# Cross-entropy backward: from two DMA queues and whole rows to one queue and sets of every fourth partition

## The chip, the cores and the metric

The kernel runs on one core of a Trainium2 chip. The metric is device time in microseconds. Before the change it is 1248.48, the median of three runs from 1247.92 to 1248.65. A profile of one further execution, with its trace, belongs to it.

## The reference

The gradient of a cross-entropy loss with respect to the logits: a softmax over the vocabulary, less one at the label.

```python
# logits: (8, 1024, 8192) float32, labels: (8, 1024) int32
logits_max = np.max(logits, axis=-1, keepdims=True)
exp_logits = np.exp(logits - logits_max)
softmax = exp_logits / np.sum(exp_logits, axis=-1, keepdims=True)
one_hot[batch_idx, seq_idx, labels] = 1.0
return (softmax - one_hot).astype(np.float32)
```

The logits are 268 MB, and as much is written.

## The kernel before

The 8192 rows are cut into `B` = 32 blocks of 256 rows. A block lies on 128 partitions with `G` = 2 rows each: partition p holds rows 2p and 2p + 1 of the block, which are neighbours in memory, 32 KB each. The text calls the 128 first rows "row t0" and the 128 second ones "row t1" (64 such row steps, t = 0 to 63). The buffer `X` has `SLOTS` = 3 slots of one block; block b uses slot b % 3, and the result overwrites the logits in place. So block b + 3 can be loaded only where block b has been stored.

A row step has four parts.

- `row_max(t)`: VectorE (DVE) takes the negated maximum of 8192 elements, after the load has landed.
- `exponentials(t)`: ScalarE (ACT) replaces the row by its exponentials and sums them.
- `mark(t)`: ACT prepares the one-hot of the label in PSUM (`hot`), in two instructions: the distance of each position from the label's word, and from this a word with one byte set. There are two buffers, one per parity of t, so `mark(t + 2)` waits for `finish(t)`.
- `finish(t)`: DVE takes the reciprocal of the sum, then multiplies the row by it and subtracts the one-hot. The last two rows are finished in two halves each.

Each block's order is written out by hand. The string `ORDER` is "r" throughout: maximum of t1, finish of t0, exponentials of t1, store of t0, mark, then already the next block's first maximum, finish of t1, the next block's exponentials, store of t1, mark, and last the load of block b + 3.

Transfers go on two queues. Loads are issued by SyncE (SP), the stores by ACT. The string `LOADS` tells how a block is loaded: "s" (blocks 0 to 2) row by row in two sets of every second partition, one on SP and one on ACT; "r" row by row over all partitions; "w" the whole block in one transfer of 8 MB, where a partition's two rows are one stretch of 64 KB. `STORES` is "r" throughout. A load waits for the stores of the block three earlier that touch the same partitions and rows (`meets`). The last two rows are stored in two halves, on SP and on ACT. Every engine works in its order, so an instruction that waits holds up all behind it on the same engine.

All operations are recorded by the helper `run`, so the profile shows nearly everything at its line, L76 (L75 for a wait that stands alone).

Of the kernel before, what the change touches and what calls it, by code (L numbers as in the profile page):

```python
# [7 lines left out]
P = 128  # L8
G = 2
SLOTS = 3  # L10

LOADS = "sssrrwwwwwwwwwwwwwwwwwwwwwwwwrrr"
STORES = "rrrrrrrrrrrrrrrrrrrrrrrrrrrrrrrr"
ORDER = "rrrrrrrrrrrrrrrrrrrrrrrrrrrrrrrr"


@with_exitstack
def kernel(
# [6 lines left out]
    nc = tc.nc  # L25
# [11 lines left out]
    T = N // P  # L37
    B = T // G
# [3 lines left out]
    o_b = o_nv.rearrange("(b p j) v -> b p j v", p=P, j=G)  # L42
# [4 lines left out]
    X = const.tile([P, SLOTS, G, V], fp32)  # L47
# [11 lines left out]
    m, s, r = (const.tile([P, T], fp32, name=n) for n in ("m", "s", "r"))  # L59
# [4 lines left out]
    with tc.tile_critical():  # L64
        sem = tc.alloc_semaphore
        got = [[sem(f"got{i}{q}") for q in range(4)] for i in range(SLOTS)]
        put = [[sem(f"put{i}{q}") for q in range(4)] for i in range(SLOTS)]
# [3 lines left out]
        def run(engine, waits, counter, method, **operands):  # L71

            waits = list(dict.fromkeys(waits))
            for w in waits[:-1]:
                engine.wait_ge(*w)  # L75
            instruction = getattr(engine, method)(**operands)  # L76
            for w in waits[-1:]:
                instruction._wait_ge(*w)
            step = 16 if method == "dma_start" else 1
            instruction.then_inc(counter, step)  # L80
            count[counter.name] = count.get(counter.name, 0) + step
            return counter, count[counter.name]

        every, rows = slice(0, P), slice(0, G)
        one = [slice(j, j + 1) for j in range(G)]
        halves = [slice(i, P, 2) for i in range(2)]
        sides = [slice(i * V // 2, (i + 1) * V // 2) for i in range(2)]
        PIECES = {
            "r": [(every, js) for js in one],
            "s": [(ps, js) for js in one for ps in halves],  # L90
            "w": [(every, rows)],
        }

        def meets(a, b):
# [3 lines left out]
        loaded, stored, sides_done = {}, {}, {}  # L98
        maxed, summed, marked, finished, freed = {}, {}, {}, {}, {}

        def load(b):
            loaded[b] = []
            before = stored.get(b - SLOTS, [])
            for q, piece in enumerate(PIECES[LOADS[b]]):
                ps, js = piece
                free = [w for other, w in before if meets(piece, other)]
                queue = nc.scalar if LOADS[b] == "s" and ps == halves[1] else nc.sync
                w = run(
                    queue, free, got[b % SLOTS][q], "dma_start",
                    out=X[ps, b % SLOTS, js, :], in_=x_b[b, ps, js, :],  # L110
                )
                loaded[b].append((piece, w))

        def store(t):
            b, j = divmod(t, G)
            stored.setdefault(b, [])
            if t >= T - G:
                for i, cs in enumerate(sides):
                    w = run(
                        nc.sync if t == T - G else nc.scalar, [sides_done[t][i]], put[b % SLOTS][G * j + i],  # L120
                        "dma_start", out=o_b[b, every, one[j], cs], in_=X[every, b % SLOTS, one[j], cs],
                    )
                    stored[b].append(((every, one[j]), w))
                return
            for q, piece in enumerate(PIECES[STORES[b]]):
                ps, js = piece
                if js.stop != j + 1:
                    continue
                w = run(
                    nc.scalar, [finished[t]], put[b % SLOTS][q], "dma_start",  # L130
                    out=o_b[b, ps, js, :], in_=X[ps, b % SLOTS, js, :],
                )
                stored[b].append((piece, w))

        def row(t):
            return X[:, t // G % SLOTS, t % G, :]
# [4 lines left out]
        def row_max(t):  # L141
            b, j = divmod(t, G)
            arrived = {w[0].name: w for piece, w in loaded[b] if meets(piece, (every, one[j]))}
            maxed[t] = run(
                nc.vector, arrived.values(), dve, "tensor_reduce",
                out=m[:, t : t + 1], in_=row(t), axis=mybir.AxisListType.X, op=Alu.max, negate=True,
            )

        def exponentials(t):
            w = run(  # L150
                nc.scalar, [maxed[t]], act, "activation",
                out=row(t), in_=row(t), func=Act.Exp, bias=m[:, t : t + 1], scale=1.0,
                accum_out=s[:, t : t + 1],
            )
            summed[t] = w

        def mark(t):
            if t >= T:
                return
            w = run(  # L160
                nc.scalar, ([made] if t < G else [freed[t - G]]) + ([marked[t - 1]] if t else []), act, "activation",
                out=away[:], in_=count16[:], func=Act.Abs, bias=at(word, t), scale=1.0,
            )
            marked[t] = run(
                nc.scalar, [w], act, "activation",
                out=hot[:, t % G, :], in_=away[:], func=Act.Relu, bias=at(unit, t), scale=at(minus, t),
            )

        def finish(t):
            w = run(nc.vector, [summed[t]], dve, "reciprocal", out=r[:, t : t + 1], in_=s[:, t : t + 1])  # L170
            bytes_ = hot[:, t % G, :].bitcast(u8)
            sides_done[t] = []
            for i, c in enumerate(sides if t >= T - G else [slice(0, V)]):
                last = run(
                    nc.vector, [marked[t], w] if i == 0 else [], dve, "scalar_tensor_tensor",
                    out=row(t)[:, c], in0=row(t)[:, c], scalar=r[:, t : t + 1], in1=bytes_[:, c],
                    op0=Alu.mult, op1=Alu.subtract,
                )
                sides_done[t].append(last)
            finished[t] = freed[t] = last  # L180

        w_raw = run(nc.scalar, [], lab_got, "dma_start", out=lab_raw[:], in_=lab_bp)
        for b in range(SLOTS):
            load(b)
        w = run(nc.gpsimd, [], pool, "memset", ap=ident[:], constant=0.0)
        w_ident = run(
            nc.gpsimd, [w], pool, "affine_select",
            out=ident[:], in_=ident[:], compare_op=Alu.not_equal, fill=1.0,
# [8 lines left out]
        for j in range(G):  # L197
            w = run(
                nc.tensor, [w_ident, w_lab], pe, "transpose",
                out=lab_ps[:, j, :], in_=lab_f[:, j, :], identity=ident[:],  # L200
            )
        w = run(nc.vector, [w], dve, "tensor_copy", out=lab[:], in_=lab_ps)
        w = run(
            nc.vector, [w], dve, "tensor_scalar",
            out=part[:], in0=lab[:], scalar1=2, scalar2=None, op0=Alu.arith_shift_right,
        )
        w_word = run(
            nc.vector, [w], dve, "tensor_scalar",
            out=word[:], in0=part[:], scalar1=-1.0, scalar2=None, op0=Alu.mult,
        )  # L210
        w = run(
            nc.vector, [w_word], dve, "tensor_scalar",
            out=lab[:], in0=lab[:], scalar1=3, scalar2=None, op0=Alu.bitwise_and,
        )
        w = run(
            nc.vector, [w], dve, "tensor_copy", out=minus[:], in_=lab[:]
        )
# [3 lines left out]
            out=unit[:], in0=minus[:], scalar1=0.0, scalar2=powers[0], op0=Alu.is_equal, op1=Alu.mult,  # L221
# [21 lines left out]
        mark(1)  # L243
        for b in range(B):
            t0, t1 = b * G, b * G + 1
            nxt = t1 + 1
            if ORDER[b] == "b":
                if t0 not in maxed:
                    row_max(t0)
                    exponentials(t0)  # L250
                row_max(t1)
                exponentials(t1)
                finish(t0)
                store(t0)
                mark(t0 + G)
                finish(t1)
                store(t1)
                mark(t1 + G)
                if b + SLOTS < B:
                    load(b + SLOTS)  # L260
                continue
            if t0 not in maxed:
                row_max(t0)
                exponentials(t0)
            row_max(t1)
            finish(t0)
            exponentials(t1)
            store(t0)
            mark(t0 + G)
            ahead = nxt < T and ORDER[b + 1] == "r"  # L270
            if ahead:
                row_max(nxt)
            finish(t1)
            if ahead:
                exponentials(nxt)
            store(t1)
            mark(t1 + G)
            if b + SLOTS < B:
                load(b + SLOTS)
        for b in range(B - SLOTS, B):  # L280
            for _, w in stored[b]:
                nc.scalar.wait_ge(*w)
# [30 lines left out]
```

## Time and profile before

| | |
|---|---|
| timed runs, median of 3 | 1248.48 us (1247.92 to 1248.65) |
| profiled execution, first to last instruction (span) | 1246.6 us |
| DVE busy | 1120.2 us, 90% |
| ACT busy | 722.7 us, 58% |
| moved by DMA | 536.98 MB in 15413 packets, mean 431 GB/s |
| DMA issues | 113: loads 46, stores 66, labels 1 |

The page gives no time for the profiled execution but its span; the timed runs lie about 1.9 us above it. In the page, q1 is the queue on which SP issues and q10 the one on which ACT issues; both feed the same sixteen DMA engines. "Share of 16 engines" is the time that a queue's packets took, over sixteen times the span or the stretch asked for. A packet is counted in the stretch in which it starts, so in a short stretch the shares can add up to more or less than 100%. The chain lists the work that ended last, followed back from the end.

### The profile page before, as it was taken

What the parts mean: (1) busy time and instruction counts of PE and PEld (TensorE: products, weight loads), DVE (VectorE), ACT (ScalarE), POOL (GpSimd) and SP (SyncE); (2) the same over time, 40 slices, a digit from 0 to 9 for tenths busy, and PEclk for the clock granted to TensorE, in tenths of its full rate; (3) what the DMA queues carried; (4) which work ended last, traced back from release to release, by engine and by line L of the source; (5) the groups of instructions that cost most, each with busy time, mean ns of one, the idle gap of its engine ahead of it and who ended that gap; (6) DMA issues with size and microseconds to landing.
All of it is one profiled execution on the core that took longest, in us unless ns stands there. A gap on an engine that the chain in (4) does not pass through costs nothing.

```text
span 1246.6 us, 809 instructions
## 1 busy us (share of the span) xinstructions
PE 0.4 (0%) x2; PEld 0.3 (0%) x2; DVE 1120.2 (90%) x208; ACT 722.7 (58%) x257; POOL 2.3 (0%) x7
## 2 busy tenths in 40 slices
PE   0000000000000000000000000000000000000000
PEld 0000000000000000000000000000000000000000
DVE  5999998889988889888898888998889988899995
ACT  2866664556555565465655655556556555566662
POOL 0000000000000000000000000000000000000000
DMA  9999999999999999999999999999999999999998
GB/s 406 413 431 434 437 432 444 435 437 421 433 429 437 443 423 433 434 431 435 430 441 435 422 435 435 434 440 426 432 434 431 433 446 434 422 430 435 429 434 383
DMA packets 15413, 536.98 MB, mean 431 GB/s; under 512 B 1808, under 2 KB 1808, under 8 KB 1840
## 3 DMA queue, kind: packets, MB, share of 16 engines
q10 hardware_dynamic: 9744, 276.89, 51.5%
q1 hardware_dynamic: 5664, 260.05, 48.3%
q14 instruction: 5, 0.04, 0.0%
HBM read 268.50 MB, written 268.44 MB: 431 GB/s over the span
## 4 chain that ended last, share of the span: by engine, by line
DMA 59%; DVE 26%; issue 11%; ACT 3%; DVEq 0%; ACTq 0%; SPq 0%
DMA X<-in_logits_dram 33%; DMA out_dram<-X 26%; DVE X L76 15%; DVE m L76 10%; ACT X L76 2%; DVEq L64 0%; DVE r L76 0%; ACT hot L76 0%; ACT away L76 0%; ACTq L76 0%; DVEq L75 0%; ACTq L308 0%; SPq L64 0%
## 5 line engine op out<-in xcount | busy, mean ns | idle before, releaser
L76 ACT ACTIVATE X<-X,m 128x8192 f32<-128x8192 f32 x64 | 455.8, 7122 | 365.2 <-DVE m L76 365.2
L76 DVE TENSOR_REDUCE m<-X 128x1 f32<-128x8192 f32 x64 | 555.6, 8682 | 105.4 <-DMA X<-in_logits_dram 105.4
L76 DVE SCALAR_TENSOR_TENSOR X<-X,r,hot 128x8192 f32<-128x8192 f32 (+1 forms) x66 | 560.1, 8489 | 3.8 <-ACT hot L76 1.6
L76 ACT ACTIVATE away<-count,word 128x2048 bf16<-128x2048 int16 x64 | 128.1, 2001 | 127.0 <-DVE X L76 127.0
L76 ACT ACTIVATE hot<-away,unit,minus 128x2048 int32<-128x2048 bf16 x64 | 131.9, 2061 | 2.1
L76 ACT ACTIVATION_READ_ACCUMULATOR X<-X,m 128x1 f32 x64 | 11.9, 186 | 0.0
L76 DVE RECIPROCAL r<-s 128x1 f32<-128x1 f32 x64 | 9.8, 153 | 0.0
L76 ACT ACT_TABLE_LOAD x1 | 1.3, 1283 | 5.3 <-issue 5.3
L76 DVE CAST lab_f<-lab_raw 32x256 f32<-32x256 int32 x1 | 0.5, 536 | 2.7 <-DMA lab_raw<-in_labels_dram 2.7
L76 POOL IOTA count<- 128x2048 int16 x1 | 1.8, 1823 | 0.0
L76 DVE TENSOR_TENSOR unit<-unit,part 128x64 f32<-128x64 f32 x3 | 0.7, 225 | 0.1
L76 DVE CAST lab<-hot 128x64 int32<-128x64 f32 x1 | 0.2, 224 | 0.5 <-PE hot L76 0.5
L76 DVE TENSOR_SCALAR part<-minus 128x64 f32<-128x64 f32 x3 | 0.6, 194 | 0.1
L76 PE MATMUL hot<-ident,lab_f 32*128 32x32 f32 x2 | 0.4, 298 | 3.3 <-DVE lab_f L76 3.3
L76 PEld LDWEIGHTS hot<-ident,lab_f 32*128 32x128 f32 x2 | 0.3, 192 | 3.3 <-DVE lab_f L76 3.3
L76 DVE CAST minus<-lab 128x64 f32<-128x64 int32 x1 | 0.2, 195 | 0.0
L76 DVE TENSOR_SCALAR word<-part 128x64 f32<-128x64 int32 x1 | 0.2, 195 | 0.0
L76 DVE TENSOR_SCALAR lab<-lab 128x64 int32<-128x64 int32 x1 | 0.2, 195 | 0.0
L76 DVE TENSOR_SCALAR unit<-minus 128x64 f32<-128x64 f32 x1 | 0.2, 195 | 0.0
L76 DVE TENSOR_SCALAR part<-lab 128x64 int32<-128x64 int32 x1 | 0.2, 194 | 0.0
L76 DVE TENSOR_SCALAR minus<-unit 128x64 f32<-128x64 f32 x1 | 0.2, 194 | 0.0
L76 POOL TENSOR_SCALAR_AFFINE_SELECT ident<-ident 32x32 f32<-32x32 f32 x1 | 0.2, 203 | 0.1
(5 smaller groups left out, 0.5 us busy)
## 6 DMA issues: line engine op xcount, KB each, us to landing
out_dram<-X ACTq DMA_DIRECT2D x62, 4096.0 KB, 30.4
X<-in_logits_dram SPq DMA_DIRECT2D x10, 4096.0 KB, 28.1
X<-in_logits_dram SPq DMA_DIRECT2D x6, 2048.0 KB, 32.6
X<-in_logits_dram ACTq DMA_DIRECT2D x6, 2048.0 KB, 37.1
out_dram<-X SPq DMA_DIRECT2D x2, 2048.0 KB, 12.7
out_dram<-X ACTq DMA_DIRECT2D x2, 2048.0 KB, 11.9
X<-in_logits_dram SPq DMA_DIRECT2D x24, 33.4
lab_raw<-in_labels_dram ACTq DMA_DIRECT2D x1, 64.0 KB, 1.8
```

The costliest lines, as they stand in the source:

```text
L76: instruction = getattr(engine, method)(**operands)
```

## The change

- All loads of logits and all stores are issued by SP. ACT issues only the load of the labels.
- Blocks 0 to 2 are loaded row by row over all partitions ("r"). All later blocks are loaded, and blocks 0 to 28 are stored, in four sets ("q"): set q holds the partitions q, q + 4, q + 8 and so on, 32 of them, with both rows, 2 MB. The last three blocks are stored by rows, and the very last one in halves of rows.
- `move(b)` runs once per block, after both rows are finished. It issues the stores of block b and the loads of block b + 3 in the order of `TURN`. The load of set q waits for the store of set q alone.
- The computation goes by block: both maxima and exponentials, then both finishes and marks. The next block's first maximum no longer comes ahead of the second finish.

```diff
-LOADS = "sssrrwwwwwwwwwwwwwwwwwwwwwwwwrrr"
-STORES = "rrrrrrrrrrrrrrrrrrrrrrrrrrrrrrrr"
-ORDER = "rrrrrrrrrrrrrrrrrrrrrrrrrrrrrrrr"
+SETS = 4
+TURN = [('S', 0), ('S', 1), ('L', 0), ('S', 2), ('L', 1), ('S', 3), ('L', 2), ('L', 3)]
+LOADS = "rrrqqqqqqqqqqqqqqqqqqqqqqqqqqqqq"
+STORES = "qqqqqqqqqqqqqqqqqqqqqqqqqqqqqrrr"
...
-        halves = [slice(i, P, 2) for i in range(2)]
+        sets = [slice(i, P, SETS) for i in range(SETS)]
...
-            "s": [(ps, js) for js in one for ps in halves],
-            "w": [(every, rows)],
+            "q": [(ps, rows) for ps in sets],
...
-        def load(b):
+        def load(b, only=None):
...
             for q, piece in enumerate(PIECES[LOADS[b]]):
+                if only is not None and q != only:
+                    continue
                 ps, js = piece
                 free = [w for other, w in before if meets(piece, other)]
-                queue = nc.scalar if LOADS[b] == "s" and ps == halves[1] else nc.sync
                 w = run(
-                    queue, free, got[b % SLOTS][q], "dma_start",
+                    nc.sync, free, got[b % SLOTS][q], "dma_start",
...
-        def store(t):
+        def store(b, only=None):
...
                 w = run(
-                    nc.scalar, [finished[t]], put[b % SLOTS][q], "dma_start",
+                    nc.sync, [finished[b * G + js.stop - 1]], put[b % SLOTS][q], "dma_start",
                     out=o_b[b, ps, js, :], in_=X[ps, b % SLOTS, js, :],
                 )
...
+        def move(b):
+            if b + SLOTS >= B:
+                store(b)
+                return
+            for what, q in TURN:
+                if what == "S":
+                    store(b, q)
+                else:
+                    load(b + SLOTS, q)
...
             row_max(t1)
+            exponentials(t1)
             finish(t0)
-            exponentials(t1)
-            store(t0)
             mark(t0 + G)
-            ahead = nxt < T and ORDER[b + 1] == "r"
-            if ahead:
-                row_max(nxt)
             finish(t1)
-            if ahead:
-                exponentials(nxt)
-            store(t1)
             mark(t1 + G)
-            if b + SLOTS < B:
-                load(b + SLOTS)
+            move(b)
```

More of the change, by code (lines that the diff above doesn't have):

```diff
@@ L99 @@
         maxed, summed, marked, finished, freed = {}, {}, {}, {}, {}
-        def load(b):
-            loaded[b] = []
+        def load(b, only=None):
+            loaded.setdefault(b, [])
             before = stored.get(b - SLOTS, [])
             for q, piece in enumerate(PIECES[LOADS[b]]):
+                if only is not None and q != only:
+                    continue
                 ps, js = piece
                 free = [w for other, w in before if meets(piece, other)]
-                queue = nc.scalar if LOADS[b] == "s" and ps == halves[1] else nc.sync
                 w = run(
-                    queue, free, got[b % SLOTS][q], "dma_start",
+                    nc.sync, free, got[b % SLOTS][q], "dma_start",
                     out=X[ps, b % SLOTS, js, :], in_=x_b[b, ps, js, :],
@@ L112, in load @@
                 loaded[b].append((piece, w))
-        def store(t):
-            b, j = divmod(t, G)
+        def store(b, only=None):
             stored.setdefault(b, [])
[L117 to L123, printed above, removed]
+            if b == B - 1:
+                for t in (T - G, T - 1):
+                    j = t % G
+                    for i, cs in enumerate(sides):
+                        w = run(
+                            nc.sync, [sides_done[t][i]], put[b % SLOTS][G * j + i],
+                            "dma_start", out=o_b[b, every, one[j], cs], in_=X[every, b % SLOTS, one[j], cs],
+                        )
+                        stored[b].append(((every, one[j]), w))
                 return
             for q, piece in enumerate(PIECES[STORES[b]]):
+                if only is not None and q != only:
+                    continue
                 ps, js = piece
-                if js.stop != j + 1:
-                    continue
                 w = run(
-                    nc.scalar, [finished[t]], put[b % SLOTS][q], "dma_start",
+                    nc.sync, [finished[b * G + js.stop - 1]], put[b % SLOTS][q], "dma_start",
                     out=o_b[b, ps, js, :], in_=X[ps, b % SLOTS, js, :],
@@ L245 @@
             t0, t1 = b * G, b * G + 1
[L246 to L251, printed above, removed]
-                exponentials(t1)
-                finish(t0)
-                store(t0)
-                mark(t0 + G)
-                finish(t1)
-                store(t1)
-                mark(t1 + G)
-                if b + SLOTS < B:
-                    load(b + SLOTS)
-                continue
             if t0 not in maxed:
@@ L265 @@
             row_max(t1)
+            exponentials(t1)
             finish(t0)
-            exponentials(t1)
-            store(t0)
             mark(t0 + G)
-            ahead = nxt < T and ORDER[b + 1] == "r"
-            if ahead:
-                row_max(nxt)
             finish(t1)
-            if ahead:
-                exponentials(nxt)
-            store(t1)
             mark(t1 + G)
-            if b + SLOTS < B:
-                load(b + SLOTS)
+            move(b)
         for b in range(B - SLOTS, B):
```

## The prediction

> **What bounds the kernel now.** The page first: its head, engine shares, DMA slices, queues and chain.
>
> ```profile
> span 1246.6 us, 809 instructions
> PE 0.4 (0%) x2; PEld 0.3 (0%) x2; DVE 1120.2 (90%) x208; ACT 722.7 (58%) x257; POOL 2.3 (0%) x7
> DMA  9999999999999999999999999999999999999998
> DMA packets 15413, 536.98 MB, mean 431 GB/s; under 512 B 1808, under 2 KB 1808, under 8 KB 1840
> q10 hardware_dynamic: 9744, 276.89, 51.5%
> q1 hardware_dynamic: 5664, 260.05, 48.3%
> DMA 59%; DVE 26%; issue 11%; ACT 3%; DVEq 0%; ACTq 0%; SPq 0%
> ```
>
> DVE looks busiest among the engines at 90%, but the two DMA queues together held all sixteen DMA engines for 51.5 + 48.3 = 99.8% of the span. Queue q1 is SP's and q10 is ACT's. So the bytes set the time, not a chain of waits. The chain that ended last (the fence's last line, 59% DMA and 26% DVE) only tells whom each block waited for.
>
> How long is a packet? The DMA view, cut to two stretches. From 276.0 to 279.6 only stores were moving, from 279.4 to 281.0 the first packets of the next load began:
>
> ```profile
> q10 hardware_dynamic: 48, 1.57, 101.1%
> ...
> q1 hardware_dynamic: 16, 1.05, 151.2%
> ```
>
> A store packet has 1.57 MB / 48 = 32 KB and took 1.011 x 3.6 x 16 / 48 = 1.213 us; a load packet has 64 KB and took 1.512 x 1.6 x 16 / 16 = 2.419 us. (A packet is counted where it starts, so a share can pass 100%.) Direction doesn't matter, only bytes, and a large packet saves next to nothing: 2 x 1.213 - 2.419 = 0.007 us.
>
> Now the work of one DMA engine, counted from the code, each of the sixteen taking 8 of a row's 128 packets. Loads: eight blocks in 32 KB packets, 128 of them, and 24 blocks in 64 KB packets, 192. Stores: 62 rows, 496 of 32 KB, and two rows in 16 KB packets, worth 32 x 0.61. That is 624 x 1.213 + 192 x 2.419 + 19.5 = 1240.9 us. Beside these stand 1808 packets under 512 B, 16 for each of 113 transfers. A stretch from 58.69 to 61.9, used again below, prices them:
>
> ```profile
> q10 hardware_dynamic: 32, 1.05, 104.9%
> q1 hardware_dynamic: 16, 0.00, 0.3%
> ```
>
> 16 of them took 0.003 x 3.21 x 16 / 16, about 0.01 us each. With 113 x 0.008 (the 0.3% is rounded) the sum is 1241.8 us. The other 4.8 us of the span are its two ends, in the windows:
>
> ```profile
> 0.00:2.00 2.00, 0.00 (x0) 0.00 (x0) 0.00 (x0) 0.00 (x0) 1.18 (x7) 1.00 0.02 7
> ...
> 1240.00:1245.00 5.00, 0.00 (x0) 0.00 (x0) 0.00 (x0) 0.00 (x0) 0.00 (x0) 1.00 0.68 292
> 1245.00:1247.00 2.00, 0.00 (x0) 0.00 (x0) 0.00 (x0) 0.00 (x0) 0.00 (x0) 1.00 0.00 0
> ```
>
> 2 us before the first data, 1.6 us after 1245, and (1 - 0.68) x 5 = 1.6 us while some DMA engines had finished and others not. 1241.8 + 5.2 is 0.4 over the span; the account closes. The timed runs' median, 1248.48, is 1.9 above this span; I take that offset as kept.
>
> **The change part by part.** *Packets.* All stores of 29 blocks and all loads of 29 blocks become 64 KB packets: 464 x 2.419 = 1122.4. Left in 32 KB packets are three blocks of loads and two of stores, 80 x 1.213 = 97.0, and the last block's 19.5. Sum 1238.9, a gain of 2.0 us. Transfers grow from 113 to 6 + 232 + 4 + 4 + 1 = 247, so the small packets cost 247 x 0.008 = 2.0, 1.1 more. Net: **-0.9 us**; if a small packet is 0.01, -0.6.
>
> *Sets of every fourth partition.* 32 partitions are two packets per engine if all sixteen share them equally. No row shows such a set. The nearest are the first loads of before, in sets of every second partition, from 20 to 44 us:
>
> ```profile
> DMA packets 396, 10.42 MB, mean 434 GB/s; under 512 B 78, under 2 KB 78, under 8 KB 78
> ```
>
> 434 GB/s, against 431 for the whole: stride 2 costs nothing, and I take nothing for stride 4.
>
> *Order by block.* The groups give DVE's and ACT's instructions:
>
> ```profile
> L76 ACT ACTIVATE X<-X,m 128x8192 f32<-128x8192 f32 x64 | 455.8, 7122 | 365.2 <-DVE m L76 365.2
> L76 DVE TENSOR_REDUCE m<-X 128x1 f32<-128x8192 f32 x64 | 555.6, 8682 | 105.4 <-DMA X<-in_logits_dram 105.4
> L76 DVE SCALAR_TENSOR_TENSOR X<-X,r,hot 128x8192 f32<-128x8192 f32 (+1 forms) x66 | 560.1, 8489 | 3.8 <-ACT hot L76 1.6
> L76 ACT ACTIVATE away<-count,word 128x2048 bf16<-128x2048 int16 x64 | 128.1, 2001 | 127.0 <-DVE X L76 127.0
> L76 ACT ACTIVATE hot<-away,unit,minus 128x2048 int32<-128x2048 bf16 x64 | 131.9, 2061 | 2.1
> L76 DVE RECIPROCAL r<-s 128x1 f32<-128x1 f32 x64 | 9.8, 153 | 0.0
> ```
>
> A block on DVE: two maxima, then two finishes, 2 x 8.68 + 2 x 8.75 + 2 x 0.15 = 35.2 us (8.75 is 560.1 / 64). The exponentials (7.1 plus 0.2 each) lie under the second maximum and the first finish; ACT's marks, 2 x 4.1, lie under the second finish and the next maximum. DVE has no gap of its own. DMA needs 16 packets x 2.419 = 38.7 us per block, so DVE has 3.5 to spare. The start: six row loads fill SP's queue from 2 us to 60.2 (48 x 1.213). Row 1 is there at 21.4, its maximum ends at 30.1; ACT does the first two marks before the second exponential, 27.7 to 35.9, so that one ends at 43.2, and the second finish at 52.1. The first store is therefore issued 8 us before the queue runs dry. Block 1 is done at 87.3 and needed at 98.9, block 2 at 122.5 and 137.6, and the distance grows. The end: after the last load come the stores of blocks 29 and 30, 38.8 us, while block 31 needs 35.2 on DVE and its first half only 22. Cost nothing. If that cover went, DVE's own row rate would decide: 35.2 x 32 = 1126, still under the DMA sum.
>
> *One queue, each load behind its store.* SP's order is S0 S1 L0 S2 L1 S3 L2 L3, then the next block. L0 waits until S0 has landed; only S1 is then queued on the DMA engines, 2 x 2.419 = 4.84 us. L1 and L2 have two sets ahead, 9.7 us. L3 waits for S3 with only L2 ahead. Everything behind a waiting load on SP waits with it: the next store too, which DVE finished long before. So there are two tight places per block, 58 in 29 blocks, each with 4.84 us of cover for the way from landing to the next first packet. The chain shows the landing and the next issue 0.02 us apart, and the issues show a small load's whole trip:
>
> ```profile
> 249.39 26.64 DMA out_dram<-X
> 276.02 0.02 issue
> 276.04 32.65 DMA X<-in_logits_dram
> ...
> lab_raw<-in_labels_dram ACTq DMA_DIRECT2D x1, 64.0 KB, 1.8
> ```
>
> 1.8 us on an idle queue. From above: that load was issued at 276.04, and up to 279.6 no q1 packet stands in the first stretch above, so 3.6 us under load. By 281.3 all sixteen had started theirs:
>
> ```profile
> q10 hardware_dynamic: 48, 1.57, 68.7%
> q1 hardware_dynamic: 16, 1.05, 45.7%
> ```
>
> 5.3 us at most, 0.4 over the cover: between 0 and 58 x 0.4 = 23 us. I take 0: the 3.6 passed behind 48 store packets, three per engine and 3 x 1.213 = 3.64 us, which looks like packets already fetched from the other queue; in one queue those are the cover itself.
>
> *Loads and stores turn about in one queue.* Before, each queue keeps one direction; after, SP's turns from loads to stores three times per block and once at the start, 88 times, and back 87 times. Before shows one such turn, on ACT's queue, when its last starting load is followed by its first store:
>
> ```profile
> 44.56 0.37 ACTq L76 DMA_DIRECT2D out_dram<-X  x1
> ...
> out_dram<-X ACTq DMA_DIRECT2D x1, 4096.0 KB, 28.1
> ```
>
> It landed at 44.56 + 28.1 = 72.7, and eight packets of 1.213 earlier is 63, so the stretch from 58.69 to 61.9 above holds the last loads. Its 32 packets took 1.049 x 3.21 x 16 / 32 = 1.684 us each instead of 1.213, two per engine: 0.94 us lost. That is one case, and SP's queue ran dry at the same moment. Against it, the engines pass from a packet of one queue to an opposite one of the other all through the steady part at full packet speed. Price of a turn to stores: 0 to 0.94 us, so 0 to 83 in all. Turns back to loads have no row; they can give the same back, if a store is merely longer on its way, or cost it again: -82 to +82. I take 0 for both, by the many rows at full speed against the one slow one, with doubt.
>
> The Trainium skill speaks against this part: Perfetto Trace Analysis, section DMA Optimizations, says it may make sense to give inputs to one issuing engine and outputs to another. It gives no figure; before's 99.8% agrees with it, and the sum here goes by the packets, which are alike on both queues.
>
> Sum: 1246.6 - 0.9 = 1245.7 span, **1247.6 us** timed. A measurement of this kernel can tell about 0.2%, 2.5 us, from no change, so this is no change.
>
> **The rivals.** *The turns cost (slower).* One mechanism: within one queue the DMA engines drain before the direction changes. From (2.5 + 0.9) / 88 = 0.04 us per turn to stores it decides; at half of 0.94 it gives 1247.6 + 41 = 1289, at the full price 1331. For it: the one row; against it: its coincidence with the dry queue. The skill's rule above would be this case.
>
> *The tight places show (slower).* The queue runs dry before L0 and L3: up to 1247.6 + 23 = 1271; it decides from 3.4 / 58 = 0.06 us each. DMA digits of 9 would remain, since 0.4 in 19 us is 2%.
>
> *Sets collide (slower).* If stride 4 makes two DMA engines take the same place in memory at a time, sets run at half speed: 232 x 4.84 = 1123 us more, 2371. The 434 GB/s at stride 2 speak against it. The Trainium skill, SBUF — State Buffer, section on the DMA port swizzle, says that bandwidth depends on how many of 16 ports the partitions reach; every fourth partition reaches all of them by its table, which leaves only the pairing of engines and ports open.
>
> *Ends close up (faster).* Waiting for all engines at each set keeps them level: the ragged 1.6 us go, and the 0.94 of the slow stretch may too: 1247.6 - 2.5 = 1245.1. Little else can go: at 99.8% there is no idle time to win, which is why no large gain is on the list.
>
> *The change does not do what it says:* stores not ready in time and the queue idle. The 8 us at the start and 3.5 per block speak against it; I count it under the tight places.
>
> **How the numbers follow.** Forecast 0.45 (of it 0.33 within 0.2%, 0.10 faster where a packet or an end is a little better, 0.02 slower); turns 0.25; tight places 0.15; collisions 0.05; ends close up 0.10. Faster 0.10 + 0.10 = 0.20, same 0.33, slower 0.02 + 0.25 + 0.15 + 0.05 = 0.47. The cases lie on both sides: the forecast's own range is 1245 to 1250. The whole range goes from 1244.5 to 1290, the turns at half price; above lie 0.12 of the turns and the 0.05 of collisions, below it 0.03.
>
> **What would show it.** Packets near 13,200 with 3952 small ones, nearly all on q1; q1 at 99.8% again and DVE idle 3.5 us per block before the first maximum, released by a load, if the forecast holds. Mean packet time well over 2.419 us per 64 KB means turns or collisions: slow packets only next to a turn are the first, all of them the second. Packets at 2.419 but a DMA share under 0.99, in gaps after L2 and S1, are the tight places. The forecast is wrong from 1251.0 up and from 1246.0 down.

## The result, and the profile after

The changed kernel takes 1322.72 us (median of 4 runs, 1316.90 to 1328.65) against 1248.35 before: a ratio of 1.059, 95% interval 1.0573 to 1.0613, 74 us slower. The forecast was 1247.6, the range 1244.5 to 1290. Where runs of one kernel lie more than 1.5% apart, its ratio is of the quicker ones alone.

The page of the changed kernel: span, engines, DMA slices, packets and queues, the chain, and two groups.

```profile
span 1315.1 us, 1029 instructions
PE 0.4 (0%) x2; PEld 0.3 (0%) x2; DVE 1120.3 (85%) x208; ACT 722.7 (55%) x257; POOL 2.3 (0%) x7
DMA  9999999999999999999999999999999999999998
DMA packets 13208, 537.02 MB, mean 408 GB/s; under 512 B 3952, under 2 KB 3952, under 8 KB 3984
q1 hardware_dynamic: 13152, 536.89, 99.3%
DMA 78%; DVE 12%; issue 4%; SPq 3%; ACT 2%; DVEq 0%
L77 DVE TENSOR_REDUCE m<-X 128x1 f32<-128x8192 f32 x64 | 553.0, 8680 | 159.0 <-DMA X<-in_logits_dram 159.0
L77 ACT ACTIVATE X<-X,m 128x8192 f32<-128x8192 f32 x64 | 455.8, 7122 | 353.4 <-DVE m L77 353.4
```

DVE and ACT do the same work in the same time. The bytes are the same. The DMA engines still count as busy for 99.3% of the span, but move 408 GB/s instead of 431. So no engine starves in the sense of an idle share; packets take longer. Which ones? A packet starts where the one before it on the same DMA engine ends, so the trace falls apart into sixteen chains, and along each chain the packets come in the order in which SP issued the transfers. That gives nearly every packet its place in a block. Its time over 2.418 us, with any gap ahead of it, is, for the two packets of a set, on average:

| S0 | S1 | L0 | S2 | L1 | S3 | L2 | L3 | block |
|---|---|---|---|---|---|---|---|---|
| 0.08 | 0.05 | **0.91** | 0.07 | 0.16 | 0.01 | 0.04 | **1.07** | 2.38 us |

29 blocks at 2.38 make 69 us; the spans differ by 1315.1 - 1246.6 = 68.5. The loss is all there, and five sixths of it stand at L0 and L3, the two loads that are issued with one set ahead of them. (Where two engines end a packet at the same moment the chains can be mixed up, so the places are good to about 0.05 us.)

One block in the trace. SP's issues in the timeline (start, duration, engine, line, operation and tiles):

```profile
187.54 0.51 SPq L77 DMA_DIRECT2D X<-in_logits_dram  x1
188.09 0.59 SPq L77 DMA_DIRECT2D out_dram<-X  x1
192.38 0.51 SPq L77 DMA_DIRECT2D X<-in_logits_dram  x1
192.93 0.60 SPq L77 DMA_DIRECT2D out_dram<-X  x1
```

L0 is issued at 187.54, when S0 has landed. The DMA view of 179.84 to 189.61, in which S0 and S1 move:

```profile
DMA packets 98, 4.20 MB, mean 430 GB/s; under 512 B 33, under 2 KB 33, under 8 KB 33
```

and of 189.62 to 195.25, in which L0 moves (packets, MB, share):

```profile
q1 hardware_dynamic: 46, 2.10, 105.3%
```

The stores run at 430 GB/s. L0 has 32 large packets (2.10 MB) that took 1.053 x 5.63 x 16 / 32 = 2.96 us each, 0.55 over the 2.42 that a packet needs: 1.1 us lost at one place.

The same block shows that less than a whole set lay ahead. L0 is issued at 187.54 and its first packet starts at 189.62, so S1 had 2.1 us left on the engine that was furthest ahead, not 4.84. S0 counts as landed when the last of sixteen engines has written its part. In this block S0's packets end on the first engine at 184.68 and on the last at 187.19, and SP issues 0.35 us after that.

By the same count the price goes with this. L0 and L3 make 58 such places in 29 blocks. The table has the work that the middle one of the sixteen engines still has when the load is issued, and what the place loses:

| left at the issue | places | lost, mean |
|---|---|---|
| 3.5 us and more | 6 | 0.3 us |
| 3 to 3.5 | 10 | 0.5 us |
| 2.5 to 3 | 15 | 0.8 us |
| 2 to 2.5 | 21 | 1.3 us |
| under 2 us | 6 | 1.7 us |

In the first block the engines are nearly level; 4.1 us are left at L0 and 3.9 at L3, and they lose 0.13 and 0.18. From the fourth block on they have drifted apart. The rate shows it: 434 GB/s from 60 to 99, about the first block, and 400 (last number) from 1195 to 1225.

```profile
DMA packets 394, 16.91 MB, mean 434 GB/s; under 512 B 128, under 2 KB 128, under 8 KB 128
1195.00:1225.00 30.00, 0.00 (x0) 0.00 (x0) 22.75 (x5) 11.73 (x7) 0.00 (x0) 1.00 1.01 400
```

The runs with one late place per block and with small packets, below, have the same relation. It is a relation within runs: one with engines kept level was not made, and why they drift is open.

### The profile page after: what moved, and what is told of

Same layout as the page of the kernel before. It is cut to its first block, busy times and chain, and to the rows that moved or that the text cites. A ratio compares the mean times of both kernels' runs of the same rounds, so it can differ in the third digit from the quotient of the medians.

```text
span 1315.1 us, 1029 instructions
## 1 busy us (share of the span) xinstructions
PE 0.4 (0%) x2; PEld 0.3 (0%) x2; DVE 1120.3 (85%) x208; ACT 722.7 (55%) x257; POOL 2.3 (0%) x7
## 2 busy tenths in 40 slices
DMA packets 13208, 537.02 MB, mean 408 GB/s; under 512 B 3952, under 2 KB 3952, under 8 KB 3984
## 3 DMA queue, kind: packets, MB, share of 16 engines
q1 hardware_dynamic: 13152, 536.89, 99.3%
## 4 chain that ended last, share of the span: by engine, by line
DMA 78%; DVE 12%; issue 4%; SPq 3%; ACT 2%; DVEq 0%
DMA out_dram<-X 77%; DVE m L77 6%; DVE X L77 5%; SPq L77 3%; DMA X<-in_logits_dram 2%; ACT X L77 1%; ACT hot L77 0%; ACT away L77 0%; DVE r L77 0%; DVEq L76 0%; SPq L296 0%; SPq L65 0%
```

## Experiments

Two theories. *Late loads:* a load that is issued with only one set ahead of it costs about 1.3 us, (74.4 + 0.9) / 58. *Turns:* each turn from loads to stores within a queue costs 0.86, (74.4 + 0.9) / 88. L0 and L3 are both late and followed by a store, so the trace of the changed kernel alone doesn't decide; L1, which is followed by a store but issued with two sets ahead, speaks for lateness.

**A store and a load in strict turn, four sets ahead.**

```diff
-TURN = [('S', 0), ('S', 1), ('L', 0), ('S', 2), ('L', 1), ('S', 3), ('L', 2), ('L', 3)]
+TURN = [('S', 0), ('P', 2), ('S', 1), ('P', 3), ('S', 2), ('L', 0), ('S', 3), ('L', 1)]
...
+                elif b:                      # "P": the load of the block before
+                    load(b + SLOTS - 1, q)
...
```

The "P" lines belong to two of the later experiments too.

> One queue, a store and a load of a set in strict turn: four turns from loads to stores per block instead of three, but each load is issued with four sets (19 us) ahead of it instead of one. Late loads (1.3 us at each of the 58 places where only one set is ahead): no such place is left, 1247 to 1251. Turns (0.86 us at each of 88): 116 turns, 1247 + 100 = 1347. A turn that costs only what the third turn of a block shows in the trace after (0.15 us): 1265.

1252.3 us, ratio 1.0038 (1.0025 to 1.0052). Of its page:

```profile
DMA packets 13208, 537.02 MB, mean 430 GB/s; under 512 B 3952, under 2 KB 3952, under 8 KB 3984
q1 hardware_dynamic: 13152, 536.89, 99.7%
```

The same packets on the same one queue, with more turns, at 430 GB/s. Turns at 0.86 us are out: 116 of them cost 4.7 us over the forecast at most, 0.04 each.

**Stores first, then loads.**

```diff
+TURN = [('S', 0), ('S', 1), ('S', 2), ('S', 3), ('L', 0), ('L', 1), ('L', 2), ('L', 3)]
```

> One queue, the four stores of a block and then its four loads: one turn per block, and each load is issued with three sets (14.5 us) ahead. Late loads: 1247 to 1250. Turns at 0.86 us: 29 of them, 1272.

1253.5 us, ratio 1.0039 (1.0026 to 1.0052). A quarter of the strict turn's turns, and the same time. Both kernels move the same sets, so sets of every fourth partition don't collide either.

**One late load per block, with no store right behind it.**

```diff
+TURN = [('S', 0), ('S', 1), ('L', 0), ('P', 2), ('P', 3), ('S', 2), ('S', 3), ('L', 1)]
```

> One queue, one load per block issued with only one set ahead of it, and loads, not a store, follow it; two turns per block from loads that were issued early. Late loads at 1.3 us: 29 places, 1285, and the slow packets are those of the late load. Turns at 0.86 us: 58, 1297, and the slow packets are those before a store. If both are needed at once (a late load right ahead of a store): 1248.

1286.2 us, ratio 1.0299 (1.0278 to 1.0320): late loads called 1285. With none, one and two late places per block the kernel takes 1252, 1286 and 1323. The guess on the packets was half wrong: by the same count, L0 loses 0.29 us, P2 0.05, P3 0.61, and S2 0.12. Lateness of the first load is paid mostly at the end of that run of loads, where the store follows: here too the blocks in which L0 was issued with little work left are those in which L0 and P3 lose most. A slow packet next to a turn is thus no proof that the turn is its cause.

**No cover at all.**

```diff
+TURN = [('S', 0), ('L', 0), ('S', 1), ('L', 1), ('S', 2), ('L', 2), ('S', 3), ('L', 3)]
```

> One queue, each load right behind the store of its set, so that nothing else is queued while it waits: 4 such places per block, 116 in all. Late loads, if what a load needs is a fixed way from landing to first data: with one set of cover (4.84 us) a place cost 1.3 us, so the way is about 6.1 us and this costs 116 x 6.1 = 710, 1960. If the 6.1 holds only behind other packets and an idle queue is quicker (1.8 us for the small load of the labels, 3 with the landing): 116 x 3 = 350, 1600. Turns alone (four per block): 1347.

1735.5 us, ratio 1.390 (1.3881 to 1.3927): (1735.5 - 1247.6) / 116 = 4.2 us a place, under the 6.1 and over the 3 that I gave. Here the queue does run dry, as its share on the page shows:

```profile
q1 hardware_dynamic: 13152, 536.89, 84.6%
```

At one place the timeline has the load's issue, at 675.95:

```profile
675.95 0.48 SPq L77 DMA_DIRECT2D X<-in_logits_dram  x1
```

The window from 675.9 to 677.2 (DMA share and GB/s are its last two numbers) has no packet:

```profile
675.90:677.20 1.30, 0.00 (x0) 0.00 (x0) 1.30 (x1) 0.00 (x0) 0.00 (x0) 1.00 0.00 0
```

And the DMA view of 675.8 to 683.7 has this load's packets:

```profile
q1 hardware_dynamic: 32, 2.10, 86.3%
```

About 1.3 us pass between the issue and the first packet, with nothing moving. The 32 packets then took 0.863 x 7.9 x 16 / 32 = 3.41 us each, 0.99 too long, 2.0 per DMA engine. So about half of the 4.2 are slow packets; of the other 2.2, 1.3 is this wait, and about 0.8 is the time from an engine's last store packet to the load's issue (0.4 on the engine that ends last).

**Two sets of cover.**

```diff
+TURN = [('S', 0), ('S', 1), ('S', 2), ('L', 0), ('S', 3), ('L', 1), ('L', 2), ('L', 3)]
```

> One queue, order S0 S1 S2 L0 S3 L1 L2 L3: the first and the last load of a block have two sets (9.7 us) ahead of them instead of one, the two others three; two turns per block. Late loads: the cover is over the 6.1 us that after suggests, so 1249 to 1256. If two sets are still too few at the old price of 1.3 us: 1323.

1252.1 us, ratio 1.0030 (1.0019 to 1.0040). L0 of one block in the DMA view, 153.6 to 158.6:

```profile
q1 hardware_dynamic: 48, 2.10, 98.9%
```

0.989 x 5.0 x 16 / 32 = 2.47 us a packet. `S2` moved ahead of `L0` and `S3` ahead of `L1` (which gives L3 its second set) are nearly the whole difference between 1323 and 1252. The engines drift apart here as well, by about 5 us, so of the 9.7 us over 5 are left on the middle engine when L0 is issued; that is enough.

**Two pieces of 4 MB in strict turn.**

```diff
-SETS = 4
+SETS = 2
+TURN = [('S', 0), ('P', 1), ('S', 1), ('L', 0)]
...
```

> One queue, two sets (every second partition, 4 MB) instead of four, a store and a load in strict turn, 19 us ahead of each load: half the transfers and half the turns of the strict turn of four sets, which ran at 1252.3. If the 4 to 5 us that are left there come from the number of turns or transfers: 1249 to 1250.5. If they come from something else, such as DMA engines that drift apart: 1252 again.

1251.7 us, ratio 1.0027 (1.0017 to 1.0036). Half the transfers and turns, the same time as the strict turn of four sets: the 3 to 4 us over the kernel before don't come from the number of transfers. The end of this run, in windows of 5 us (their length; busy time of PE, PEld, DVE, ACT and POOL; granted clock; DMA share; GB/s):

```profile
1240.00:1245.00 5.00, 0.00 (x0) 0.00 (x0) 0.00 (x0) 0.00 (x0) 0.00 (x0) 1.00 0.61 262
1245.00:1250.00 5.00, 0.00 (x0) 0.00 (x0) 0.00 (x0) 0.00 (x0) 0.00 (x0) 1.00 0.16 69
```

Before, the share was 0.68 from 1240 to 1245 and nothing after; here a few DMA engines work on after 1245. Some lag at the end is part of the rest. What makes them lag is open.

**The packets' size at the same cover.**

```diff
-SETS = 4
+SETS = 2
-            "q": [(ps, rows) for ps in sets],
+            "q": [(ps, js) for js in one for ps in sets],
```

> One queue and the changed kernel's order S0 S1 L0 S2 L1 S3 L2 L3, but the four pieces of a block are one row of every second partition each: still 2 MB and 4.84 us of cover at two places per block, now four packets of 32 KB per DMA engine instead of two of 64 KB. If what counts is the time of cover: 58 places at 1.3 us, near 1322 again. If what counts is how many packets stand ahead of the late load: four are enough, 1250 to 1257.

1320.2 us, ratio 1.0565 (1.0547 to 1.0582), as with large packets. What counts is the time of the work ahead, not the number of packets.

**Eight pieces of 1 MB, 7.3 us of cover.** (Each load is again issued behind the store of its place; semaphores for eight pieces are added.)

```diff
-            "q": [(ps, rows) for ps in sets],
+            "q": [(ps, js) for js in one for ps in sets],
+TURN = [('S', 0), ('S', 1), ('S', 2), ('S', 3), ('L', 0), ('S', 4), ('L', 1), ('S', 5),
+        ('L', 2), ('S', 6), ('L', 3), ('S', 7), ('L', 4), ('L', 5), ('L', 6), ('L', 7)]
```

> One queue, eight pieces of 1 MB (one row of every fourth partition, two packets of 32 KB per DMA engine), each load three pieces behind the store of its place: the first and the last load of a block have 7.3 us of cover, the others more; five turns per block. No cover cost 4.2 us a place, 4.84 us cost 1.3, 9.7 us cost under 0.1. If the cost falls evenly between the last two: 58 x 0.65 = 38, 1287. If the need ends near 6 us: 1252 to 1258.

1325.6 us, ratio 1.0613 (1.0597 to 1.0629): neither. By the count of packets L0 is nearly free at 0.03 us, but L7, the other watched load, loses about 0.3, so where the need ends isn't shown; on the middle engine 4.5 to 4.9 us of work were left at the two, not 7.3. Most of the pieces from L1 to S7 lose 0.15 to 0.4 us each, although L2 and L3 were issued with 10 us and more left. In all it is 2.7 us a block, (1325.6 - 1247.6) / 29:

```profile
DMA packets 24346, 537.05 MB, mean 405 GB/s; under 512 B 7664, under 2 KB 7664, under 8 KB 7696
q1 hardware_dynamic: 24288, 536.90, 99.8%
```

This queue changes direction every 2.4 us over much of a block, the strict turn of four sets every 4.8 us, and that one loses nothing like it. Size of piece and of packet were changed together here, so that a price of turns at small pieces is a rival that stands; neither theory explains this run.

**Two queues with the sets.**

```diff
-                    nc.sync, [finished[b * G + js.stop - 1]], put[b % SLOTS][q], "dma_start",
+                    nc.scalar, [finished[b * G + js.stop - 1]], put[b % SLOTS][q], "dma_start",
```

> Stores go back to ACT's queue; the sets of every fourth partition, the order by block and the order of the loads on SP stay. If it is the one queue that costs 74 us, by late loads or by turns from loads to stores, this runs at 1247 to 1250, since no queue turns and no store stands behind a waiting load. If the sets collide or the order by block costs, it stays near 1320.

Ratio 1.0075 (1.0055 to 1.0096), from runs of 1257.2 and 1259.5 us; two others took 1351 and 1355. So the one queue was most of the loss, but two queues with sets aren't as good as before either, by 9 us. I expected 1250 at most. The profile is of the run of 1355 us and can't tell what the 9 us are; that is open.

**The order by block alone**, in the kernel before.

```diff
-ORDER = "rrrrrrrrrrrrrrrrrrrrrrrrrrrrrrrr"
+ORDER = "bbbbbbbbbbbbbbbbbbbbbbbbbbbbbbbb"
```

> The kernel before, with nothing changed but the order of the computation: by block. If this order costs nothing, as DVE's 3.5 us to spare per block say: 1248.4. If it is why two queues with sets ran at 1257: 1255 or more.

1248.2 us, ratio 0.9999 (0.9989 to 1.0008). The order is free.

**Whole blocks stored in one transfer**, on two queues, order by block.

```diff
-STORES = "rrrrrrrrrrrrrrrrrrrrrrrrrrrrrrrr"
-ORDER = "rrrrrrrrrrrrrrrrrrrrrrrrrrrrrrrr"
+STORES = "wwwwwwwwwwwwwwwwwwwwwwwwwwwwwrrr"
+ORDER = "bbbbbbbbbbbbbbbbbbbbbbbbbbbbbbbb"
```

> Two queues as before the change, order by block, and each block stored in one transfer of 8 MB with 64 KB packets, as it is loaded: 84 transfers instead of 113, 232 packets per DMA engine for 464. By packet durations this saves 2 us: 1246. If 64 KB packets on both queues are why two queues with sets ran at 1257: 1255 or more. A block's load now waits for the whole store; both queues are empty of other work then, so that late loads could cost here too, 4.2 x 24 = 100 at most, 1347.

Four runs from 1295.5 to 1320.2 us, ratio 1.0425 (1.0379 to 1.0471). Larger packets and fewer transfers, and 53 us slower by the ratio. Part of it is a hole near the end, in which DVE and ACT work on the last blocks and little moves; the windows:

```profile
1260.00:1265.00 5.00, 0.00 (x0) 0.00 (x0) 5.00 (x1) 1.53 (x2) 0.00 (x0) 1.00 0.08 33
1265.00:1270.00 5.00, 0.00 (x0) 0.00 (x0) 4.96 (x3) 3.18 (x1) 0.00 (x0) 1.00 0.03 13
```

Earlier there are slow packets too. In one block the next load is issued at 563.97 and the next store at 565.35; the packets of SP's queue that start from 564 to 569, which belong to the load before, take mostly 3.0 to 4.0 us instead of 2.4. It fits that work that comes late costs on two queues as well; no run here tests it alone.

## Why the prediction was wrong

*What bounds the kernel:* right. The DMA engines are busy for 99.3% of the span after as well, with DVE at 85%, and most packets of 64 KB still take 2.418 us.

*Packets, -0.9 us:* 13208 packets and 3952 small ones came as counted. The gain didn't: the best kernels on one queue stand at 1251.7 to 1253.5, 4 to 6 us over the 1247.6, with a longer ragged end as one part and the rest open. The rival *ends close up* is refuted by the same end.

*Sets, order by block, start:* right at nothing, within those 4 to 6 us (1252 with the sets on one queue, 0.9999 for the order).

*The tight places:* **this is the step that failed.** The two places per block were found, and that everything on SP waits behind them. Their price was put at 0 to 0.4 us and taken as 0. It is 1.3 us on average, 75 in all; with one such place per block it is half, and with two sets ahead next to nothing. Three arguments led there.

First, the cover of 4.84 us was a whole set's time, as if all engines were level and the landing cost nothing. When L0 and L3 are issued, about 2.7 us are left on the middle engine. The prediction had read 3.6 to 5.3 us from a load's issue to its first packets; against 2.7 that is 0.9 to 2.6 us short, and 1.3 lies in it. In the first block, where about 4 us are left, the places do cost under 0.2 us. Second, the 3.6 us was read as three packets of the other queue, which in one queue would be cover. No run says whether that reading was right. Third, the cover was set against the time to the *first packet*, as if a load that arrives before the queue is dry loses nothing. Without any cover about half of the 4.2 us goes into packets that take 3.4 instead of 2.4 us. For the same reason I looked for gaps and a DMA share under 0.99; the share was 99.3%, and the loss lay mostly inside the packets. What lengthens them isn't settled, nor why engines with 4 to 5 us left at such a place still lose something.

*The turns:* the rival at full price gave 1331, close to the result, and for the wrong reason. The one row it rested on, 0.94 us lost where the first run of loads ends, needs another reading: that run began on an idle queue, and as in the experiment with one late load the debt may be paid where the run ends. That reading fits and wasn't tested. So the nearness of 1331 was luck. My test in the trace, "slow packets only next to a turn", would have confirmed the wrong theory. The Trainium skill (Perfetto Trace Analysis, DMA Optimizations) says that it may make sense to give inputs and outputs an issuing engine each, for a more dynamic spread. At pieces of 2 MB two are not needed here: with loads issued early, 116 turns in one queue ran at 1.0038. With these late loads the second queue does help (1.0075 against 1.059), perhaps because a waiting load then holds up no store; that reason wasn't tested.

*Chances:* slower had 0.47, most of it on the turns. The range ended at the turns' half price and left out the result.

## What to carry to other kernels

Where a transfer waits for another to land, count the work that is already queued on the DMA engines behind the one it waits for, and count it from the engine that ends last. In this kernel nothing queued cost 4.2 us a place; one set, 4.84 us on paper and about 2.7 at the issue, still 1.3; two sets, 9.7 on paper and over 5 at the issue, next to nothing. Moving two stores per block ahead of waiting loads took 70 us off. A DMA share near 100% doesn't show such losses: compare GB/s, or a packet's time with that of the same packet elsewhere.

## What the runs showed of the hardware that was not expected

A late load lengthens packets and leaves few gaps: 2.96 us for 64 KB instead of 2.42 in the block shown, at a DMA share of 99.3% over the run. The sixteen DMA engines drift apart, in the run with two sets from 0.7 us at the first L0 to about 5, and a transfer lands with the last of them.

After an idle queue the first packets start about 1.3 us after the start of the issue, which itself takes 0.48. The Trainium skill (DMA: Bandwidth & Descriptors, section on latency and other measured facts) gives about 0.6 us to the first byte on this path; counted like this, the trace has twice that here. And pieces of 1 MB, half of them in turn with stores every 2.4 us, lose 2.7 us per block, which no run here explains.
